# A hybrid encoder layer on one core: GpSimd's half of a sum put behind VectorE's, a small sum moved to GpSimd, one reciprocal a turn later

## The chip, the cores and the metric

The kernel runs on one core of a Trainium2 chip. The metric is the device time in microseconds (us) of one execution. Inside the core, TensorE (PE, with its weight loads as PEld), VectorE (DVE), ScalarE (ACT) and GpSimd (POOL) work in parallel, each through its own queue in order; SyncE (SP) issues all the DMAs here, in order too. An instruction that waits for another engine holds up everything behind it in its own queue.

## What is computed

One encoder layer is applied to two sequences with shared weights: a short one of 1024 tokens ("prompt") and a long one of 2048 ("sample"). The projected features go through three groups, each multiplied with its own SiLU gate, and their concatenation goes through an output projection, an RMS norm and a residual sum. Cut to what matters here:

```python
h = rms_norm(x, norm_pre)
z = h @ w_in                       # u_pool, g_pool, q, k, v, g_attn, q_x, g_x
pool_out = multiscale_pool(u_pool) * silu(g_pool)
# 8 query heads on 2 key/value heads, over all tokens
p = softmax(q @ k.T * 64 ** -0.5)
attn_out = (p @ v) * silu(g_attn)
# 4 heads over 256 memory tokens
x_out = memory_attention(q_x, k_m, v_m) * silu(g_x)
mix = concatenate([pool_out, attn_out, x_out])
y = mix @ w_out
out = x + rms_norm(y, norm_post)
```

All of it is float32; matrix products that need more than one pass' precision are split into a high and a low part (hi, lo), so that one product is three matmuls.

## The kernel before

The first part of the span, up to some 700 us, computes the projections of both sequences and stores queries, keys, values and gates to DRAM. The second part, which the change touches, is attention, output projection and the closing norm.

The second part goes through **pairs** of row blocks (256 tokens), eight of the sample and then four of the prompt. Each pair has three **groups**: kind 0 and kind 1 are self-attention on one key/value head each, kind 2 is the memory attention. After the first pair the order is 0, 2, 1. A group goes through its keys in **chunks** of 128 (16 in the sample, 8 in the prompt, 2 for the memory). Two chunks make a **turn**, and one loop over all turns of all groups writes out the order of every engine by hand (a manual schedule). Work that isn't tied to the loop is put into a table of due turns with `at(turn, f, ...)`, and `due(turn)` in the loop takes from it what is due; a fraction of a turn tells where inside the turn that is. In one turn the loop does:

- `look` (twice): TensorE computes a tile N of scores for a group to come (L186, L178 for the memory), and VectorE takes its negated row maxima (L191). The tile N has one buffer, so that the next N waits for this maximum. When all of a group are there, `shift` turns them into rows.
- `weights` (for two chunks): TensorE accumulates the scores S (L213, L221), and ScalarE takes the exponential into a tile P (L223). P has five buffers.
- `sums`: adds the chunk's P onto the group's z, column by column (L235 on GpSimd for the first 512 of 1024 columns, L236 on VectorE for the rest; `CUT = (0, 512)` says that in the prompt VectorE adds all of it). The first chunk of the turn is added in this turn, the second one in the next, between its two looks.
- `project`: one to four steps of the output projection of an earlier pair (`Output.piece`, L380 to L382, which read the tile mix).
- `values`: P times the values into acc (L248), every second turn for four chunks.
- `totals`: a turn after a group's last chunk, TensorE adds up z over the partitions (L257). It needs both halves of the last sum.

A group then goes on by due turns: `take` multiplies acc with the gate (L263, VectorE); `turned` and `inverse` transpose the totals, take the reciprocal (L272) and transpose back into a tile gz of one buffer (L267, L275, all VectorE), and store it to DRAM (L277); `spread` loads it back, broadcast over partitions (L282); `mix_out` multiplies the gated values with it (L292, GpSimd), and later ScalarE and GpSimd split the product into hi and lo (L295, L299) as the tile mix. The pooling branch of the pair goes through the same two lines as "pu". For the projected rows, `square` takes the sum of squares on ScalarE (L386), `scale` multiplies with the gain on VectorE (L398), `norm` makes the inverse root (L402 a sum of two numbers and epsilon on VectorE, L405 a power on GpSimd), and `out` scales and adds the residual (L414 on ScalarE and L415 on GpSimd; L411 on VectorE for the very last pair).

Of the kernel before, what the change touches and what calls it, by code (L numbers as in the profile page):

```python
# [10 lines left out]
ALU = mybir.AluOpType  # L11
# [6 lines left out]
EPS = 1e-6  # L18
# [5 lines left out]
def encoder(ctx, tc, I, O):  # L24


    nc = tc.nc
# [26 lines left out]
    make_identity(nc, ident)  # L54
    mhalf = const.tile([128, 8], F32, name="mhalf")
    nc.vector.memset(mhalf, -0.5)

    def rsqrt(pool, ss, n, count, tag):

        r = pool.tile([128, n], F32, name="rs", tag=tag)  # L60
        nc.vector.tensor_scalar(out=r, in0=ss, scalar1=1.0 / count, scalar2=EPS,  # L61
                                op0=ALU.mult, op1=ALU.add)
        nc.gpsimd.tensor_tensor(out=r, in0=r, in1=mhalf[:, 0:n], op=ALU.pow)  # L63
        return r
# [66 lines left out]
    class Group:  # L131
# [93 lines left out]
        def sums(self, k):  # L225
            if k == 0:
                return
            if k == 1:
                self.z = dbl.tile([128, 2, 512], F32, name="z", tag="z")
            flat = "p j q -> p (j q)"  # L230
            z, P = self.z.rearrange(flat), self.P[k].rearrange(flat)
            a = self.P[0].rearrange(flat) if k == 1 else z
            cut = CUT[self.s]
            if cut:
                nc.gpsimd.tensor_tensor(out=z[:, :cut], in0=a[:, :cut], in1=P[:, :cut], op=ALU.add)  # L235
            nc.vector.tensor_tensor(out=z[:, cut:], in0=a[:, cut:], in1=P[:, cut:], op=ALU.add)  # L236

        def values(self, ks):

# [107 lines left out]
    class Output:  # L347
# [51 lines left out]

        def norm(self):  # L400
            s1 = dbl.tile([128, 1], F32, name="s1", tag="s1")
            nc.vector.scalar_tensor_tensor(out=s1, in0=self.ss[:, 0:1], scalar=EPS, in1=self.ss[:, 1:2],  # L402
                                           op0=ALU.add, op1=ALU.add)
            self.r = dbl.tile([128, 1], F32, name="rs", tag="rsy")
            nc.gpsimd.tensor_tensor(out=self.r, in0=s1, in1=mhalf[:, 0:1], op=ALU.pow)  # L405

# [36 lines left out]
    later = {}  # L443

    def at(turn, f, *args):

        later.setdefault(round(turn, 2), []).append((f, args))
# [5 lines left out]
    first = {}  # L453
# [7 lines left out]
    for pair in pairs:  # L461
        ends = [first[g] + g.chunks // 2 - 1 for g in pair.groups]
        begin = first[pair.groups[0]]
        at(begin + 5.2, pair.load_pool)
        pair.free = begin + (6 if pair.last else HOLD[pair.s])
        at(begin + 7, pair.pool, begin + 7)
        for g in pair.groups:
            wait = first[g] + g.chunks // 2 + (2 if pair.last else 3)
            if pair is pairs[0] and g.kind != 1:
                wait += 3  # L470
            at(wait + 0.6, g.mix_out, wait + 1, pair)
        at(max(ends) + (3 if pair.last else 7), open_fill, pair)
    value_runs, sums_at = {}, {}
    for g in groups:
        n, c = first[g], g.chunks // 2
        g.early = g in pairs[0].groups
        at(n + (1.2 if g.kind == 1 and g.s == 0 else 0.2), g.load_late)
        k = 0
        while k < c:
            run = 1 if 2 < n + k < first[pairs[1].groups[0]] + 6 else 2  # L480
            value_runs[n + k + run - 1] = g, list(range(2 * k, min(2 * k + 2 * run, 2 * c)))
            k += run
        at(n + max(c, run) + 0.1, g.take)
        sums_at[n + c] = g
        at(n + c + 1.1, g.turned)
        if g in pairs[-1].groups:
            at(n + c + (1.4 if g.kind < 2 else 2.1), g.inverse)
            at(n + c + (1.4 if g.kind < 2 else 2.1), g.spread)
        else:
            at(n + c + (1.4 if g.kind < 2 else 2.6), g.inverse)  # L490
            at(n + c + (2.1 if g.kind < 2 else 3.1), g.spread)
    for c in range(NC):
        at(int(2.5 * c + 1), load_w_out, c)
        for h in range(2):
# [15 lines left out]
    looks, n = {}, len(turns)  # L510
# [31 lines left out]
    with ExitStack() as p1:  # L542
        one = p1.enter_context(tc.tile_pool(name="p1one", bufs=1))
# [437 lines left out]
    with tc.manual_schedule(engines=order):  # L981
        turn = 0
        while turn < len(turns) or later or fill:
            g, k = turns[turn] if turn < len(turns) else (None, 0)
# [66 lines left out]
```

## Time and profile before

| | before |
|---|---|
| median of 3 runs | 1746.3 us (1745.69 to 1746.43) |
| the profiled execution | 1745.43 us, span 1743.6 us |
| PE busy | 1697.3 us (97%) |
| DVE busy | 1116.8 us (64%) |
| POOL busy | 844.3 us (48%) |
| ACT busy | 656.7 us (38%) |
| granted TensorE clock, mean | 0.996 |

Read the rows of the profile like this. A row of a group has the line in the code, the engine, the operation, the tiles that it writes and reads with their shapes, the count, then the busy time in us and the mean in ns of one, and behind the second bar the engine's idle time just before them and what ended it. A row of the timeline begins with its start and its length in us; where rows in a row are equal they are merged ("x2"), and in square brackets stands the idle time of the engine before it and what ended that. A row of the waits names who waited for whom, then us in total, times, and the longest. A row of the windows has the stretch in us, its length, then the busy us of each engine with the count of instructions (PE, PEld, DVE, ACT, POOL), the granted TensorE clock, the share of the DMA engines and GB/s.

### The profile page before, as it was taken

What the parts mean: (1) busy time and instruction counts of PE and PEld (TensorE: products, weight loads), DVE (VectorE), ACT (ScalarE), POOL (GpSimd) and SP (SyncE); (2) the same over time, 40 slices, a digit from 0 to 9 for tenths busy, and PEclk for the clock granted to TensorE, in tenths of its full rate; (3) what the DMA queues carried; (4) which work ended last, traced back from release to release, by engine and by line L of the source; (5) the groups of instructions that cost most, each with busy time, mean ns of one, the idle gap of its engine ahead of it and who ended that gap; (6) DMA issues with size and microseconds to landing.
All of it is one profiled execution on the core that took longest, in us unless ns stands there. A gap on an engine that the chain in (4) does not pass through costs nothing. (4 is left out here: it accounts for less than half of the span.)

```text
span 1743.6 us, 25303 instructions
## 1 busy us (share of the span) xinstructions
PE 1697.3 (97%) x9400; PEld 1168.0 (67%) x9400; DVE 1116.8 (64%) x1434; ACT 656.7 (38%) x978; POOL 844.3 (48%) x778
## 2 busy tenths in 40 slices
PE   7899999999999999999999999999999999999998
PEld 6889889798898986544555555555555555566566
DVE  6754316552164424799878787877777757876862
ACT  5533225332252211445444344444343433443441
POOL 4555205570054610499666575767666663331331
PEclk9999999999999999999999999999999999999999
DMA  7643634436443393612121212112111143323222
GB/s 256 177 132 87 186 94 135 128 89 172 113 124 91 110 217 85 181 62 86 49 73 61 68 53 76 56 49 77 48 58 55 61 127 110 103 80 109 68 91 91
DMA packets 151851, 178.27 MB, mean 102 GB/s; under 512 B 20896, under 2 KB 120368, under 8 KB 151728
## 3 DMA queue, kind: packets, MB, share of 16 engines
q1 hardware_dynamic: 151728, 176.65, 34.0%
q8 instruction: 74, 1.21, 0.3%
q14 instruction: 49, 0.40, 0.1%
HBM read 121.26 MB, written 55.20 MB: 101 GB/s over the span
## 5 line engine op out<-in xcount | busy, mean ns | idle before, releaser
L191 DVE TENSOR_REDUCE nb<-N 128x2 f32<-128x1024 f32 x320 | 390.3, 1220 | 215.7 <-PE N L186 215.0
L223 ACT ACTIVATE P<-S 128x1024 f32<-128x1024 f32 x344 | 334.6, 1023 | 436.5 <-PE S L221 174.0
L235 POOL TENSOR_TENSOR z<-z,P 128x512 f32<-128x512 f32 x224 | 324.2, 1447 | 160.2 <-ACT P L223 140.4
L248 PE MATMUL acc<-P,V 128*64 128x512 f32 (+1 forms) x1472 | 320.3, 575 | 1.5
L236 DVE TENSOR_TENSOR z<-z,P 128x512 f32<-128x512 f32 (+1 forms) x272 | 269.3, 990 | 4.5 <-ACT P L223 4.3
L614 PE MATMUL pz<-hT_hi,w_hi 128*128 128x512 f32 x592 | 235.2, 397 | 1.7 <-ACT vmst L884 0.8
L615 PE MATMUL pz<-hT_lo,w_hi 128*128 128x512 f32 x592 | 232.8, 393 | 0.0
L616 PE MATMUL pz<-hT_hi,w_lo 128*128 128x512 f32 x592 | 231.5, 391 | 0.1
L248 PEld LDWEIGHTS acc<-P,V 128*64 128x64 f32 x1472 | 95.3, 137 | 170.7 <-issue 130.7
L221 PE MATMUL S<-q,DH 64*128 64x512 f32 x1280 | 201.6, 392 | 0.0
L63 POOL TENSOR_TENSOR rs<-rs,mhalf 128x4 f32<-128x4 f32 (+2 forms) x76 | 83.6, 1103 | 210.4 <-DVE rs L61 207.3
L186 PE MATMUL N<-KH,q 64*128 64x512 f32 x640 | 157.0, 487 | 12.4 <-DVE nb L191 11.0
L186 PEld LDWEIGHTS N<-KH,q 64*128 64x128 f32 x640 | 59.8, 183 | 153.2 <-DVE nb L191 86.4
L614 PE MATMUL pz<-w_hi,hT_hi 128*128 128x384 f32 (+1 forms) x416 | 141.6, 341 | 3.8 <-ACT hT_hi L68 3.8
L615 PE MATMUL pz<-w_lo,hT_hi 128*128 128x384 f32 (+1 forms) x416 | 140.7, 338 | 0.9 <-DVE w_lo L69 0.8
L616 PE MATMUL pz<-w_hi,hT_lo 128*128 128x384 f32 (+1 forms) x416 | 140.6, 339 | 0.0
L380 PE MATMUL py<-wo_hi,mix 128*128 128x512 f32 x336 | 139.0, 414 | 0.0
L69 DVE TENSOR_TENSOR w_lo<-wraw,w_hi 128x3072 fp32r<-128x3072 f32 (+2 forms) x21 | 67.8, 3227 | 107.3 <-ACT w_hi L68 106.9
L221 PEld LDWEIGHTS S<-q,DH 64*128 64x128 f32 x1280 | 120.1, 185 | 23.6 <-issue 2.4
L382 PE MATMUL py<-wo_hi,mix 128*128 128x512 f32 x336 | 131.6, 392 | 0.1
L381 PE MATMUL py<-wo_lo,mix 128*128 128x512 f32 x336 | 131.5, 391 | 0.0
L614 PEld LDWEIGHTS pz<-hT_hi,w_hi 128*128 128x128 f32 x592 | 111.1, 188 | 29.1 <-issue 4.5
(152 smaller groups left out, 2436.3 us busy)
## 6 DMA issues: line engine op xcount, KB each, us to landing
wraw<-w_in SPq DMA_DIRECT2D x15, 1536.0 KB
dg<-gst SPq DMA_DIRECT2D x48, 256.0 KB
q<-dq SPq DMA_DIRECT2D x24, 512.0 KB
gz<-rows SPq DMA_DIRECT2D x72, 128.0 KB
x<-x_sample SPq DMA_DIRECT2D x16, 512.0 KB
xr<-x_sample SPq DMA_DIRECT2D x16, 512.0 KB
y_sample<-xr SPq DMA_DIRECT2D x32, 256.0 KB
dq<-qst SPq DMA_DIRECT2D x96, 64.0 KB
```

The costliest lines, as they stand in the source:

```text
L186: nc.tensor.matmul(S[:, 512 * j:512 * j + 512], lhsT=self.q[h, 0, 128 * lane:128 * lane + 128], rhs=KH[self.kind][h, 512 * a:512 * a + 512 ...
L191: nc.vector.tensor_reduce(out=out, in_=S, axis=AX.X, op=ALU.max, negate=True)
L221: nc.tensor.matmul(S[:, at + x:at + x + w], lhsT=K, rhs=self.q[h, qx, x:x + w], start=False, stop=n == 2, skip_group_check=True)
L223: nc.scalar.activation(out=self.P[k].rearrange("p j q -> p (j q)"), in_=S, func=AF.Exp)
L235: nc.gpsimd.tensor_tensor(out=z[:, :cut], in0=a[:, :cut], in1=P[:, :cut], op=ALU.add)
L236: nc.vector.tensor_tensor(out=z[:, cut:], in0=a[:, cut:], in1=P[:, cut:], op=ALU.add)
L248: nc.tensor.matmul(self.acc[64 * j:64 * j + 64, x], lhsT=v, rhs=P[:, j, x], start=(k, i) == (0, 0), stop=k == self.chunks - 1, skip_group_ ...
L380: nc.tensor.matmul(ps, lhsT=mh, rhs=wo_hi[:, c, cols], start=first, stop=False)
L382: nc.tensor.matmul(ps, lhsT=ml, rhs=wo_hi[:, c, cols], start=False, stop=final)
L614: nc.tensor.matmul(ps, lhsT=sh, rhs=mh, start=c == 0, stop=False)
L615: nc.tensor.matmul(ps, lhsT=sh, rhs=ml, start=False, stop=False)
L616: nc.tensor.matmul(ps, lhsT=sl, rhs=mh, start=False, stop=c == n - 1)
```

## The change

It has three parts. In `sums`, VectorE's half is now issued first, and GpSimd's half is given a dependency on it, except for a group's last chunk. In `norm`, the sum of two numbers and epsilon is done by GpSimd's tensor_scalar, ahead of the power there. For the memory group of every pair, `inverse` comes 0.8 turns later and `spread` one turn later (not in the last pair), and `mix_out` one turn later (not in the first pair and not in the last).

```diff
+    def behind(later, first):
+        tc.add_manual_dep(later.ins, first.ins.name,
+                          mybir.DependencyInfo(mybir.DependencyClass.Sync, mybir.DependencyReason.DATA),
+                          reason="one after the other")
...
             cut = CUT[self.s]
+            v = nc.vector.tensor_tensor(out=z[:, cut:], in0=a[:, cut:], in1=P[:, cut:], op=ALU.add)
             if cut:
-                nc.gpsimd.tensor_tensor(out=z[:, :cut], in0=a[:, :cut], in1=P[:, :cut], op=ALU.add)
-            nc.vector.tensor_tensor(out=z[:, cut:], in0=a[:, cut:], in1=P[:, cut:], op=ALU.add)
+                e = nc.gpsimd.tensor_tensor(out=z[:, :cut], in0=a[:, :cut], in1=P[:, :cut], op=ALU.add)
+                if k < self.chunks - 1:
+                    behind(e, v)
...
             s1 = dbl.tile([128, 1], F32, name="s1", tag="s1")
-            nc.vector.scalar_tensor_tensor(out=s1, in0=self.ss[:, 0:1], scalar=EPS, in1=self.ss[:, 1:2],
-                                           op0=ALU.add, op1=ALU.add)
+            nc.gpsimd.tensor_scalar(out=s1, in0=self.ss[:, 0:1], scalar1=EPS, scalar2=self.ss[:, 1:2],
+                                    op0=ALU.add, op1=ALU.add)
...
             if pair is pairs[0] and g.kind != 1:
                 wait += 3
+            elif g.kind == 2 and not pair.last:
+                wait += 1
             at(wait + 0.6, g.mix_out, wait + 1, pair)
...
         else:
-            at(n + c + (1.4 if g.kind < 2 else 2.6), g.inverse)
-            at(n + c + (2.1 if g.kind < 2 else 3.1), g.spread)
+            at(n + c + (1.4 if g.kind < 2 else 3.4), g.inverse)
+            at(n + c + (2.1 if g.kind < 2 else 4.1), g.spread)
```

The lines of the changed kernel are some 5 to 7 higher than before's from `sums` on. In the rows below, a bracket names the engines or DMA queues whose semaphores the instruction waits for.

The first place is GpSimd's queue at the end of a kind 0 group of the sample, from the mix of the pair before to the group's last two chunks. Before:

```order
L299 TENSOR_TENSOR mix<-gate,mix 128x512 [waits Activation_49]
L405 TENSOR_TENSOR rs<-s_8859,mhalf 128x1 [waits DVE_49]
L235 TENSOR_TENSOR z<-z,P 128x512 [waits Pool_49]
L235 TENSOR_TENSOR z<-z,P 128x512 [waits Activation_49,Pool_49]
L415 TENSOR_TENSOR xr<-xr,y 128x512 [waits DMAHW1_49,DMAHW6_49,DMAHW0_49,Activation_49]
L299 TENSOR_TENSOR mix<-gate,mix 128x512 x2
L292 TENSOR_TENSOR pu<-pu,pg 128x512 [waits DMAHW7_49,DMAHW1_49,DMAHW0_49]
L235 TENSOR_TENSOR z<-z,P 128x512 [waits Pool_49]
L235 TENSOR_TENSOR z<-z,P 128x512 [waits Activation_49,Pool_49]
L415 TENSOR_TENSOR xr<-xr,y 128x512 [waits Activation_49]
L235 TENSOR_TENSOR z<-z,P 128x512 [waits Pool_49]
```

And of the change:

```order
L306 TENSOR_TENSOR mix<-gate,mix 128x512 [waits Activation_49]
L409 TENSOR_SCALAR s_8859<-ssy 128x1
L412 TENSOR_TENSOR rs<-s_8859,mhalf 128x1 [waits Pool_49]
L241 TENSOR_TENSOR z<-z,P 128x512 [waits DVE_49]
L241 TENSOR_TENSOR z<-z,P 128x512 [waits DVE_49,Pool_49]
L422 TENSOR_TENSOR xr<-xr,y 128x512 [waits DMAHW1_49,DMAHW6_49,DMAHW0_49,Activation_49]
L306 TENSOR_TENSOR mix<-gate,mix 128x512 x2
L299 TENSOR_TENSOR pu<-pu,pg 128x512 [waits DMAHW7_49,DMAHW1_49,DMAHW0_49]
L241 TENSOR_TENSOR z<-z,P 128x512 [waits DVE_49,Pool_49] x2
L422 TENSOR_TENSOR xr<-xr,y 128x512 [waits Activation_49]
L241 TENSOR_TENSOR z<-z,P 128x512 [waits Pool_49]
```

The instructions keep their order; the small sum stands ahead of the power, and every sum but the last of the group waits for VectorE instead of ScalarE.

The second place is VectorE's queue behind the first chunks of the kind 1 group of the sample's last pair, where the memory group's reciprocal (RECIPROCAL, STREAM_TRANSPOSE gz) stands. Before:

```order
L236 TENSOR_TENSOR z<-P 128x512
L236 TENSOR_TENSOR z<-z,P 128x512 x3
L272 RECIPROCAL rz<-rz 128x8
L275 STREAM_TRANSPOSE gz<-rz 128x256
L191 TENSOR_REDUCE nb<-N 128x2
L236 TENSOR_TENSOR z<-z,P 128x512
L191 TENSOR_REDUCE nb<-N 128x2
L236 TENSOR_TENSOR z<-z,P 128x512
L191 TENSOR_REDUCE nb<-N 128x2
```

And of the change:

```order
L239 TENSOR_TENSOR z<-P 128x512
L239 TENSOR_TENSOR z<-z,P 128x512 x3
L196 TENSOR_REDUCE nb<-N 128x2
L239 TENSOR_TENSOR z<-z,P 128x512
L196 TENSOR_REDUCE nb<-N 128x2
L239 TENSOR_TENSOR z<-z,P 128x512
L279 RECIPROCAL rz<-rz 128x8
L282 STREAM_TRANSPOSE gz<-rz 128x256
L196 TENSOR_REDUCE nb<-N 128x2
```

Two row maxima and two sums now stand ahead of the reciprocal. In SyncE's queue the load of gz (two DMAs) goes behind the load of a following group's queries, here also behind two loads of keys.

The third place is VectorE's queue in the prompt's second pair, where the norm's small sum (s) stood ahead of a row maximum. Before:

```order
L236 TENSOR_TENSOR z<-P 128x1024
L191 TENSOR_REDUCE nb<-N 128x2
L272 RECIPROCAL rz<-rz 128x8
L275 STREAM_TRANSPOSE gz<-rz 128x256
L402 SCALAR_TENSOR_TENSOR s_13557<-ssy 128x1
L191 TENSOR_REDUCE nb<-N 128x2
```

And of the change:

```order
L239 TENSOR_TENSOR z<-P 128x1024
L196 TENSOR_REDUCE nb<-N 128x2
L279 RECIPROCAL rz<-rz 128x8
L282 STREAM_TRANSPOSE gz<-rz 128x256
L196 TENSOR_REDUCE nb<-N 128x2
```

The sum is gone from VectorE, and nothing else moved there.

## The prediction

> **What bounds the kernel now.** I read the page's busy shares first, then its groups.
>
> ```profile
> span 1743.6 us, 25303 instructions
> PE 1697.3 (97%) x9400; PEld 1168.0 (67%) x9400; DVE 1116.8 (64%) x1434; ACT 656.7 (38%) x978; POOL 844.3 (48%) x778
> L235 POOL TENSOR_TENSOR z<-z,P 128x512 f32<-128x512 f32 x224 | 324.2, 1447 | 160.2 <-ACT P L223 140.4
> ```
>
> TensorE is busy 97% of the span, so only what TensorE waits for can move the time. GpSimd's halves of the sums of weights (L235; VectorE's are L236) cost 324 us on an engine that is not the bound. The next view is TensorE's own waits, stage by stage: first between 830 and 1420 us, the long sequence's attention from the second pair of row blocks on, then between 715 and 830 us.
>
> ```profile
> engine line waited for: us in total, times, longest us
> PE acc L257 <- POOL z L235: 1.1, 4, 0.6
> ```
> ```profile
> PE N L186 <- DVE nb L191: 3.8, 7, 1.2
> ```
>
> In 590 us of steady state TensorE waits 1.1 us in all, and the one thing that it waits for is GpSimd's half of a sum (L257 adds up the finished sums). For VectorE it isn't shown waiting once. A faster VectorE therefore has nothing to win in these 590 us, and a later GpSimd has something to lose. Only in the first two groups of heads does TensorE wait for VectorE's row maxima, 3.8 us together.
>
> **Part 1: GpSimd's half behind VectorE's half.** The claim behind such an order would be that the halves disturb each other. They do:
>
> ```profile
> 1004.30 0.68 DVE L236 TENSOR_TENSOR z<-z,P 128x512 f32<-128x512 f32 x1
> ...
> 1009.53 0.68 DVE L236 TENSOR_TENSOR z<-z,P 128x512 f32<-128x512 f32 x1
> ...
> 1011.61 1.69 DVE L236 TENSOR_TENSOR z<-z,P 128x512 f32<-128x512 f32 x1
> ```
>
> VectorE's add takes 0.68 us when it comes first, and 1.69 us at 1011.61, where a GpSimd add is already running. GpSimd's queue in the same stretch, the end of one group (chunks 8 to 15 of its sum), is this:
>
> ```profile
> 999.26 2.99 POOL L235 TENSOR_TENSOR z<-z,P 128x512 f32<-128x512 f32 x2 [1.64 <-ACT P L223]
> 1004.47 1.64 POOL L235 TENSOR_TENSOR z<-z,P 128x512 f32<-128x512 f32 x1 [2.21 <-PE N L186]
> 1006.07 1.77 POOL L299 TENSOR_TENSOR mix<-pu,mix 128x512 fp32r<-128x512 f32 x1
> 1007.80 1.29 POOL L299 TENSOR_TENSOR mix<-gate,mix 128x512 fp32r<-128x512 f32 x1
> 1009.05 0.55 POOL L405 TENSOR_TENSOR rs<-s,mhalf 128x1 f32<-128x1 f32 x1
> 1009.55 3.19 POOL L235 TENSOR_TENSOR z<-z,P 128x512 f32<-128x512 f32 x2
> 1012.80 1.65 POOL L415 TENSOR_TENSOR xr<-xr,y 128x512 f32<-128x512 f32 x1
> 1014.41 2.97 POOL L299 TENSOR_TENSOR mix<-gate,mix 128x512 fp32r<-128x512 f32 x2
> 1017.33 1.27 POOL L292 TENSOR_TENSOR pu<-pu,pg 128x512 f32<-128x512 f32 x1
> 1018.56 3.12 POOL L235 TENSOR_TENSOR z<-z,P 128x512 f32<-128x512 f32 x2
> 1021.63 1.75 POOL L415 TENSOR_TENSOR xr<-xr,y 128x512 f32<-128x512 f32 x1
> 1023.35 1.28 POOL L235 TENSOR_TENSOR z<-z,P 128x512 f32<-128x512 f32 x1
> ```
> ```profile
> 927.69 1.28 POOL L235 TENSOR_TENSOR z<-z,P 128x512 f32<-128x512 f32 x1
> ```
> ```profile
> 929.03 0.64 PE L257 MATMUL acc<-z,ones 128*32 128x256 f32 x8
> ```
> ```profile
> 1024.68 0.64 PE L257 MATMUL acc<-z,ones 128*32 128x256 f32 x8 [0.19 <-POOL z L235]
> ```
> ```profile
> 1407.30 0.64 PE L257 MATMUL acc<-z,ones 128*32 128x256 f32 x8 [0.56 <-POOL z L235]
> ```
>
> From 1004.47 to the last add's end at 1024.63 GpSimd doesn't stop, and 0.05 us later TensorE starts L257, after an idle 0.19 us. This is the place without slack. It lies at the end of the first group of a pair and comes back every 96 us: the first and the last of six such starts, at 929 us (0.06 us behind GpSimd's add, too short a wait to be listed) and at 1407 us, are shown beside the one at 1024.
>
> Now the change. Chunk 9's GpSimd add is the second of the two from 999.26; it is finished by 1002.25, in time that GpSimd otherwise idles (the 2.21 us ahead of 1004.47). Behind VectorE's half, which ends at 1004.98, it starts at about 1005.1. So the busy stretch starts 0.6 us later (1005.1 against 1004.47) and has 1.25 us more in it (one add, 1.28 us, less its overlap with the next). Part 2 puts a small sum ahead of rs, some 0.35 us. That adds 2.2 us. Taken off: thirteen big instructions at 1.28 us and rs at 0.55 us would be 17.2 us, and the rows from 1004.47 sum to 20.5 us, so some 3.3 us of them is waiting for VectorE. Most of it stays, since VectorE's six adds still have to get in between. Laid out one by one, with 1.28 us for each GpSimd instruction and 0.55 us more where a VectorE add gets in first, the last add ends near 1026.1, so 1.5 us later than now. I take **+1.5 us** for each of six ends, **+9.0 us**; the bounds are 0 (all the added time given back by fewer collisions) and 2.2 us (none), 0 to 13.2 us. The last chunk is left free by the change, but it stands behind the others in GpSimd's queue, so that doesn't help.
>
> What else stands behind the delayed adds: mix (L299) and xr (L415). TensorE's projection reads the first two mix rows, the second of them two of its steps of three matmuls in:
>
> ```profile
> 1010.10 0.50 PE L380 MATMUL py<-wo_hi,mix 128*128 128x512 f32 x1
> ```
>
> They end at 1007.84 and 1009.09 and by the same lay-out come up to 1.6 us and 2.2 us later, 1009.4 and 1011.3. That is about in time, and I cost it at nothing; were the second needed at 1010.10 itself, it would be 1.2 us per pair. Buffers of weights come free later too:
>
> ```profile
> ACT P L223 <- POOL z L235: 102.8, 35, 3.9
> ```
>
> ScalarE's exponentials are named as waiting 102.8 us for GpSimd's adds. As TensorE isn't shown waiting for ScalarE once between 830 and 1420 us, that cover holds for another us or two; cost nothing.
>
> The gain of part 1 is in the first two groups: at most the 4.1 us there (3.8 us above and one more wait of 0.3 us of the same sort). In them L257 again needs GpSimd's last add, and GpSimd's queue is full, so most of an earlier VectorE is given back there; I take **-0.8 us**, bounds 0 and -4.1.
>
> The Trainium skill ("SBUF — State Buffer", section "Who interferes with whom") says that VectorE and GpSimd hold a shared port in turn for a whole instruction, and that the issue order decides who blocks. The rows agree (0.68 against 1.69 us). By that rule the order moves the waiting from one engine to the other and frees no port time, and here the engine without slack is the one that is now put second; the sum would be nearer the 13.2 us than 9.0.
>
> **Part 2: the norm's small sum on GpSimd.** It removes 24 instructions from VectorE and adds 24 to GpSimd. GpSimd has no such instruction now; the nearest rows are the power on the same 128x1 shape and a 128x8 product:
>
> ```profile
> L405 POOL TENSOR_TENSOR rs<-s,mhalf x24: 541/548/1540, 866.1 to 1738.5; 128x1 f32<-128x1 f32 x24
> ```
> ```profile
> L811 POOL TENSOR_TENSOR sm<-sm,edge 128x8 f32<-128x8 f32 x4 | 0.8, 202 | 0.2
> ```
>
> So between 0.20 and 0.55 us; I take 0.35, which is already in the stretch above. On VectorE it matters in two places, in the short sequence:
>
> ```profile
> 1553.25 1.08 DVE L402 SCALAR_TENSOR_TENSOR s<-ssy 128x1 f32<-128x1 f32 x1
> ```
> ```profile
> 1555.52 0.50 PE L186 MATMUL N<-KH,q 64*128 64x512 f32 x2 [0.89 <-DVE nb L191]
> ```
> ```profile
> 1619.73 0.50 PE L186 MATMUL N<-KH,q 64*128 64x512 f32 x2 [0.84 <-DVE nb L191]
> ```
>
> The sum, held up by GpSimd, delays the maximum behind it by 1.0 us, and TensorE idles 0.89 us; the same 64 us later, 0.84 us. Without it: **-1.7 us**.
>
> At the very end the sum stands behind two products on VectorE:
>
> ```profile
> 1736.79 0.19 ACT L386 ACTIVATION_READ_ACCUMULATOR junk<-py 128x1 f32 x1
> ```
> ```profile
> 1737.63 0.68 DVE L398 TENSOR_TENSOR y<-py,npost 128x512 f32<-128x512 f32 x1
> ...
> 1739.10 1.41 DVE L411 SCALAR_TENSOR_TENSOR xr<-y,rs,xr 128x512 f32<-128x512 f32 x2 [0.73 <-POOL rs L405]
> ```
>
> Its input is there at 1736.98. GpSimd, idle, could add (0.35) and take the power (0.55) by about 1738.0, so L411 starts near 1738.1 instead of 1739.10: **-1.0 us** (0.8 to 1.1 with the sum's bounds).
>
> **Part 3: the memory group's reciprocal a turn later.** Its instructions (reciprocal, transpose, one store, two loads, the product on GpSimd) keep their number and their spacing. What goes is a wait of VectorE for GpSimd's product of the group before:
>
> ```profile
> DVE gz L275 <- POOL gate L292: 4.1, 1, 4.1
> ```
> ```profile
> 1426.22 0.66 PE L186 MATMUL N<-KH,q 64*128 64x512 f32 x2 [2.24 <-DVE nb L191]
> ```
> ```profile
> 1426.40:1429.80 3.40, 3.40 (x10) 1.01 (x11) 3.02 (x3) 0.00 (x0) 0.74 (x1) 0.50 0.36 92
> ```
>
> The transpose L275 waits 4.1 us, the row maxima behind it are late, TensorE idles 2.24 us, and for the next 3.4 us its granted clock is 0.50, which loses half of 3.4 us. In the new order two maxima and two adds stand ahead of the reciprocal, so this stall goes whole: 2.2 + 1.7 = **-3.9 us**. In SyncE's queue the reload of gz now stands behind loads of keys and queries; the product that waits for it has nothing on TensorE behind it, so I cost it at nothing.
>
> The Trainium skill ("TensorE: Matmul & The Clock Gate", section "What's actually happening") lets the clock fall after at least one idle window of about 3.4 us. By it 2.24 us would not do, and the 1.7 us would not be gained; here the row with 0.50 decides. Another stall shows how near the edge this is:
>
> ```profile
> 328.52 0.66 PE L820 MATMUL pm<-sm,poolw 128*128 128x504 f32 x1 [2.19 <-DVE u L781]
> ```
> ```profile
> 328.50:331.90 3.40, 3.38 (x13) 2.52 (x14) 1.51 (x4) 1.06 (x3) 0.00 (x0) 1.00 0.29 60
> ```
>
> After 2.19 us idle the clock stayed at 1.00.
>
> **The sum.** +9.0 - 0.8 - 1.7 - 1.0 - 3.9 = **+1.6 us**. The profiled execution took 1745.43 us (1.8 us beside its span), 0.9 us under the median of 1746.3; on the median that is **1747.9 us**.
>
> **The rivals.** A measurement of this kernel can tell about 0.2%, 3.5 us, from no change.
> - *GpSimd catches up* (faster). If fewer collisions give back all that is added to the 20 us stretch, or if VectorE nearly always starts first already, as at 1009.53 against 1009.55, the +9.0 falls away: 1746.3 - 7.4 = 1738.9 us. For it: GpSimd's adds average 1447 ns against 1.28 us undisturbed. Against it: VectorE's six adds must still fit into the stretch.
> - *GpSimd's last add becomes TensorE's wait* (slower). Each of six ends gives the full 2.2 us, and idle times of over 2 us at L257 halve the clock at two of them, 1.7 us each: 1746.3 + 13.2 + 3.4 - 7.4 = 1755.5 us. It decides against the change from 7.4 / 6 = 1.2 us per end on. For it: L257 has no slack now. Against it: the clock held at 2.19 us idle. By the clock rule of the Trainium skill above neither the halving here nor the 1.7 us of part 3 would be there, and this case would be 1753.8 us.
>
> **How the numbers follow.** The balance (1743 to 1750) gets 0.42, GpSimd catching up 0.25, the full delay 0.33. With one case to each band: faster 0.25, same 0.42, slower 0.33. The unknowns' ends are 1746.3 - 10.7 (nothing lost, all 4.1 us gained) = 1735.6 and 1746.3 + 13.2 + 3.4 - 4.7 (0.8 at the end, 1.7 in the short sequence and only the 2.2 us) = 1758.2; leaving a tenth out on each side, the range is 1738 to 1756.
>
> **What would show it.** Right: VectorE's L236 adds near 0.7 us, GpSimd's adds near 1.3 us; TensorE idle for 1.5 us or more ahead of L257 six times, 96 us apart; no stall near 1426, 1555 and 1620; the last L411 pair some 0.6 us behind the product. Wrong: L257's waits unchanged at 0.2 us (then I mis-sized GpSimd's stretch), or TensorE waiting at L299's mix or for ScalarE's weights (then the cover that I counted on was thin).

## The result and the profile after

| | before | after |
|---|---|---|
| median | 1745.99 us (1743.88 to 1746.43, 4 runs) | 1768.65 us (1768.06 to 1772.95, 4 runs) |
| the profiled execution | 1745.43 us, span 1743.6 us | 1768.06 us, span 1766.3 us |
| mean granted TensorE clock | 0.996 | 0.990 |

The ratio is 1.0137 [1.0118, 1.0156]: the change makes the kernel slower by 1.4%, 22.7 us. The page of the changed kernel, in the rows that answer to those of before (the lines are 3 to 9 higher now: L241 is GpSimd's half of a sum, L239 VectorE's, L264 the totals, L306 the mix):

```profile
PE 1707.1 (97%) x9400; PEld 1175.8 (67%) x9400; DVE 1091.6 (62%) x1410; ACT 657.3 (37%) x978; POOL 818.3 (46%) x802
L241 POOL TENSOR_TENSOR z<-z,P 128x512 f32<-128x512 f32 x224 | 293.3, 1309 | 172.4 <-DVE z L239 159.2
```

This page alone looks like a success. GpSimd's adds fell from 1447 to 1309 ns, VectorE is busy for 25 us less, GpSimd for 26 us less. The gain of VectorE is not where the order was to bring it, though. Its adds by shape, before and after:

```profile
L236 DVE TENSOR_TENSOR z<-z,P 128x512 f32<-128x512 f32 x224 | 201.6, 900 | 4.0 <-ACT P L223 4.0
L236 DVE TENSOR_TENSOR z<-P 128x512 f32<-128x512 f32 x24 | 28.7, 1194 | 0.0
```
```profile
L239 DVE TENSOR_TENSOR z<-z,P 128x512 f32<-128x512 f32 x224 | 200.1, 893 | 4.5 <-ACT P L228 4.4
L239 DVE TENSOR_TENSOR z<-P 128x512 f32<-128x512 f32 x24 | 15.9, 661 | 0.0
```

Only the first add of each group became short (1194 to 661 ns, 12.8 us together). The other 224 take 893 ns instead of 900, and most of what is left of the 25 us are the small sums, which have gone to GpSimd. So what the order shortened are GpSimd's adds, and of VectorE's only the first of each group. The first two experiments below agree: in these two rows VectorE has 892 and 663 ns with the order alone, 859 and 1196 ns without it.

TensorE's waits over the whole span (who waited for whom; us in total, times, longest) show where the span went:

```profile
PE acc L264 <- POOL z L241: 13.3, 6, 2.7
PE N L191 <- DVE nb L196: 7.0, 13, 1.3
PE py L264 <- POOL z L241: 3.8, 2, 2.2
...
PE py L389 <- POOL mix L306: 2.9, 1, 2.9
```

The wait for GpSimd's last add of a group, 1.1 us in four waits before, is now 13.3 us in six; two more such waits (in the first pair, where the totals go into the tile py) and one for mix are new. GpSimd's queue at the same place as in the prediction, chunks 9 to 15 of a kind 0 group's sum, now reads:

```profile
1017.73 1.28 POOL L241 TENSOR_TENSOR z<-z,P 128x512 f32<-128x512 f32 x1 [2.56 <-DVE z L239]
1019.71 1.28 POOL L241 TENSOR_TENSOR z<-z,P 128x512 f32<-128x512 f32 x1 [0.69 <-DVE z L239]
...
1024.05 0.30 POOL L409 TENSOR_SCALAR s<-ssy 128x1 f32<-128x1 f32 x1
1024.44 0.84 POOL L412 TENSOR_TENSOR rs<-s,mhalf 128x1 f32<-128x1 f32 x1
1025.25 2.65 POOL L241 TENSOR_TENSOR z<-z,P 128x512 f32<-128x512 f32 x2
...
1033.71 2.98 POOL L241 TENSOR_TENSOR z<-z,P 128x512 f32<-128x512 f32 x2
1036.66 1.26 POOL L422 TENSOR_TENSOR xr<-xr,y 128x512 f32<-128x512 f32 x1
1037.89 1.25 POOL L241 TENSOR_TENSOR z<-z,P 128x512 f32<-128x512 f32 x1
```
```profile
1039.20 0.64 PE L264 MATMUL acc<-z,ones 128*32 128x256 f32 x8 [2.12 <-POOL z L241]
```

Chunk 9's add (1017.73) now waits for VectorE and opens the busy stretch. Chunk 10's add waits for VectorE once more, 0.69 us, and from 1019.71 to 1039.14 GpSimd hardly stops. TensorE starts the totals 0.06 us later, after 2.12 us idle, where it was 0.19 us. Of VectorE's adds in that stretch some are still held up, as the slowest and the one right before the stretch show:

```profile
1016.88 0.68 DVE L239 TENSOR_TENSOR z<-z,P 128x512 f32<-128x512 f32 x1
...
1033.75 1.80 DVE L239 TENSOR_TENSOR z<-z,P 128x512 f32<-128x512 f32 x1
```

The order binds the two halves of one chunk, not VectorE's add of one chunk against GpSimd's instructions of another. The add at 1033.75 is that of chunk 15 and still meets GpSimd's of chunk 13, which began at 1033.71.

The stall has an echo. The stretches right after it (length; busy us and count of PE, PEld, DVE, ACT, POOL; granted clock; DMA share; GB/s) at this end and at the next:

```profile
1040.20:1043.60 3.40, 3.40 (x20) 2.42 (x16) 2.75 (x4) 1.02 (x1) 0.18 (x1) 0.51 0.72 218
1139.20:1142.60 3.40, 3.40 (x20) 2.40 (x16) 2.75 (x4) 1.02 (x1) 0.16 (x1) 0.50 0.70 224
```

For 3.4 us the clock is half. The starts of the same instructions in both traces give the price: from the totals at 1024.68 (now 1039.20, +14.52) to those five microseconds later (1029.65, now 1045.71, +16.06) another 1.54 us go. This came at five of the six ends.

With such differences of starts the whole span can be put together:

| stretch | us | |
|---|---|---|
| first part, to 717 us | +2.1 | not the change's, see below |
| first pair and start of the second, to 833 us | +8.9 | totals late by 1.64 and 2.17 us, mix by 2.88 us, two half clocks |
| six ends of kind 0 groups | +11.1 | 1.77 to 2.06 each, from 40 us ahead of the totals to their start |
| half clocks behind five of them | +7.7 | 1.53 to 1.55 each |
| stall at 1426 us | -3.9 | gone |
| short sequence, two stalls | -1.8 | gone (0.95 and 0.88) |
| the very end | -1.0 | |
| small steps elsewhere | -0.4 | |
| sum | +22.6 | span 1743.63 to 1766.26 (the rounded rows give 22.7) |

The loss of the second pair has a place of its own. GpSimd before the mix, in the changed kernel:

```profile
808.42 1.28 POOL L241 TENSOR_TENSOR z<-z,P 128x512 f32<-128x512 f32 x1 [0.69 <-DVE z L239]
810.38 1.29 POOL L241 TENSOR_TENSOR z<-z,P 128x512 f32<-128x512 f32 x1 [0.69 <-DVE z L239]
...
813.61 1.26 POOL L241 TENSOR_TENSOR z<-z,P 128x512 f32<-128x512 f32 x1 [0.69 <-DVE z L239]
815.56 1.28 POOL L241 TENSOR_TENSOR z<-z,P 128x512 f32<-128x512 f32 x1 [0.69 <-DVE z L239]
...
827.82 1.26 POOL L306 TENSOR_TENSOR mix<-pu,mix 128x512 fp32r<-128x512 f32 x1
```
```profile
829.13 0.80 PE L389 MATMUL py<-wo_hi,mix 128*128 128x512 f32 x1 [2.88 <-POOL mix L306]
```

Four times GpSimd stands idle for 0.69 us, the length of VectorE's half, with a full queue behind it: 2.8 us. TensorE, which needs the mix at the queue's end, waits 2.88 us. In the kernel before, GpSimd's rows of this stretch show no idle time:

```profile
809.72 3.48 POOL L235 TENSOR_TENSOR z<-z,P 128x512 f32<-128x512 f32 x2
...
817.83 1.29 POOL L299 TENSOR_TENSOR mix<-pu,mix 128x512 fp32r<-128x512 f32 x1
```

### The profile page after: what moved, and what is told of

It reads as the page before. It is cut to its first block, busy times and chain, and to the rows that moved or that the text cites. A ratio compares the mean times of both kernels' runs of the same rounds, so it can differ in the third digit from the quotient of the medians.

```text
span 1766.3 us, 25311 instructions
## 1 busy us (share of the span) xinstructions
PE 1707.1 (97%) x9400; PEld 1175.8 (67%) x9400; DVE 1091.6 (62%) x1410; ACT 657.3 (37%) x978; POOL 818.3 (46%) x802
## 5 line engine op out<-in xcount | busy, mean ns | idle before, releaser
L241 POOL TENSOR_TENSOR z<-z,P 128x512 f32<-128x512 f32 x224 | 293.3, 1309 | 172.4 <-DVE z L239 159.2
L239 DVE TENSOR_TENSOR z<-z,P 128x512 f32<-128x512 f32 (+1 forms) x272 | 265.5, 976 | 5.1 <-ACT P L228 4.7
L226 PE MATMUL S<-q,DH 64*128 64x512 f32 x1280 | 206.3, 400 | 0.0
```

The costliest lines, as they stand in the source:

```text
L226: nc.tensor.matmul(S[:, at + x:at + x + w], lhsT=K, rhs=self.q[h, qx, x:x + w], start=False, stop=n == 2, skip_group_check=True)
L239: v = nc.vector.tensor_tensor(out=z[:, cut:], in0=a[:, cut:], in1=P[:, cut:], op=ALU.add)
L241: e = nc.gpsimd.tensor_tensor(out=z[:, :cut], in0=a[:, :cut], in1=P[:, :cut], op=ALU.add)
```

## The experiments

The theory at this point: part 1, the order, makes GpSimd's last adds late and brings all of the loss; parts 2 and 3 gain, except that the small sum lengthens GpSimd's queue a little. The rivals: part 2's small sum (on the full GpSimd) carries the loss; or part 3 has moved work into these places; or the loss is in the last chunks' order alone.

### Parts 2 and 3 without the order

Diff against the kernel before (with part 3 as in the change):

```diff
-            nc.vector.scalar_tensor_tensor(out=s1, in0=self.ss[:, 0:1], scalar=EPS, in1=self.ss[:, 1:2],
-                                           op0=ALU.add, op1=ALU.add)
+            nc.gpsimd.tensor_scalar(out=s1, in0=self.ss[:, 0:1], scalar1=EPS, scalar2=self.ss[:, 1:2],
+                                    op0=ALU.add, op1=ALU.add)
...
+            elif g.kind == 2 and not pair.last:
+                wait += 1
```

> Parts 2 and 3 alone: the sums of weights as before, no order between the halves. Theory (the order makes GpSimd's last add of a group late, TensorE waits for it at the totals, and some of these waits halve its clock): the waits at the six ends go back to 0.2 to 0.6 us, with 0.3 us each for the small sum on GpSimd, no half clock between 830 and 1420 us; the gains of the two parts (3.9, 1.8 and 1.0 us) stay: about 1741 us (1738 to 1744), faster than before by 0.2 to 0.4%. Rival (the small sum and the later product fill GpSimd's queue and have their share of the loss): 1752 us or more, with waits of over 1 us at the totals.

Measured: 1741.74 us (1740.53 to 1743.25, 10 runs), ratio 0.9984 [0.9975, 0.9993]. The stall at 1426 us is gone (3.87 us), no half clock stands behind a totals, and the totals wait for GpSimd:

```profile
PE acc L262 <- POOL z L240: 3.9, 6, 1.0
```

3.9 us in six against 1.1 in four. That is the small sum: 0.38 to 0.44 us at each end (the run below that takes it out of these places bears this out). So it is neither part 2 nor part 3 that makes the kernel slow, but part 2 gives back a good part of what it gains.

### The order alone

Diff against the kernel before: the new `sums` and `behind` of the change, nothing else.

> Part 1 alone: VectorE's half first and GpSimd's half behind it except for a group's last chunk; norm and reciprocals as before. Theory: the whole loss is here, and the gains of the other parts are missing: 1768.65 + 6.7 less some 2 us for the small sum that is not on GpSimd, about 1773 us (1769 to 1777), waits of 1.7 us or more at the totals, and the stall of the memory group's reciprocal near 1440 us is back. Rival (the parts need each other): 1758 us or less.

Measured: 1775.96 us (1773.37 to 1776.59, 4 runs), ratio 1.0175 [1.0159, 1.019]. Part 1 carries the loss, and alone it is worse than all three parts together. In the steady stretch (840 to 1445 us) TensorE's waits are:

```profile
PE acc L264 <- POOL z L241: 10.2, 6, 2.3
PE N L191 <- DVE nb L196: 9.4, 6, 1.6
```

The totals wait 1.57 to 1.60 us (the last 2.28), not 2.1, since the small sum isn't in GpSimd's queue. That is a little under the 1.7 us expected, and there is no half clock behind any of the six. But a second stall has come, once in every pair:

```profile
1060.41 0.45 DVE L282 STREAM_TRANSPOSE gz<-rz 128x256 f32<-128x256 f32 x1 [2.60 <-POOL gate L299]
```

It is the stall that the kernel before had only at 1426 us: VectorE's transpose waits for GpSimd's product of the group before, the row maxima behind it are late, and TensorE waits 1.57 us for them. The order delays that product in every pair. So part 3, which moves the transpose back by a turn, is what makes part 1 bearable; in the full change this stall is nowhere (part 2 is missing here too, but neither the transpose nor that product is part of it). At the place of the old stall TensorE now idles 3.07 us, with 6.83 us of half clock behind it. The time lies in the expected range partly by luck: the 7.7 us of half clock behind the totals are gone, and the 9.4 us of the second stall, which nothing had foretold, stand in their place. VectorE's half issued first, but without the dependency, was not run; the rows name the dependency, since it is VectorE's half that ends 159.2 of the 172.4 us of idle time before GpSimd's adds in the full change.

### The order in the first half of each sum

```diff
-                if k < self.chunks - 1:
+                if k < self.chunks // 2:
```

> The change, but with the order only for the first half of a group's chunks (1 to 7 of 16; none in the memory group). Theory (what counts is that GpSimd's adds of the last chunks can't be done ahead of its busy stretch): the last chunks are free, the waits at the six steady ends fall from 2.1 to 2.7 us to 0.6 us or less, no half clock there, and at least half of the 8.9 us of the first two pairs goes: 1741 to 1750 us. Rival (each ordered add costs its share through the waits on VectorE): half of the loss stays, about 1757 us.

Measured: 1748.5 us (1744.76 to 1750.45, 10 runs), ratio 1.002 [1.001, 1.003]. The steady ends are where the kernel of parts 2 and 3 has them (0.57 to 0.58 us, the last 0.97, no half clock), so the steady loss comes from the order on the last chunks. One part of the expectation was a miss: at least half of the early 8.9 us should have gone, and most of it stayed (1.76, 1.92 and 3.98 us, 7.7 together). From 715 to 1445 us:

```profile
PE acc L264 <- POOL z L241: 3.9, 6, 1.0
PE py L264 <- POOL z L241: 3.3, 2, 1.6
PE py L389 <- POOL mix L306: 2.9, 1, 2.9
```

From the first pair to the start of the second GpSimd also splits the output weights (wo_lo), and in the kernel of parts 2 and 3 it shows no idle time between 802 and 828 us in which a delay of early chunks could be made up. That this keeps the early loss is argued from those rows, not tested apart.

### The order in the first pair only

```diff
-                if k < self.chunks - 1:
+                if self.early and k < self.chunks - 1:
```

> The change, but with the order only in the first pair's three groups, where TensorE does wait for VectorE. Theory: the six steady ends are free again; in the first pair the waits at the totals (1.6 and 2.2 us in the change) stay, and with them a half clock: 1741 + 4 to 7 us, 1745 to 1749 us. Rival (the first pair's stalls in the change come from elsewhere, as the chain of projections, and the order helps VectorE there): 1741 us or less, with no wait at the first pair's totals.

Measured: 1746.51 us (1743.45 to 1750.35, 10 runs), ratio 1.0008 [0.9998, 1.0017], 4.8 us above the kernel of parts 2 and 3 on the same chip. The first pair's two late totals stay (1.64 and 2.16 us, the second with a half clock behind it), the mix is on time and the steady ends are at 0.56 to 0.61 us (the last 0.97). So the order costs in the first pair too, at the very place where VectorE's relief was to help. And the 2.88 us at the mix come from the order on the second pair's chunks, which this run leaves free.

### The change with 384 of 1024 columns on GpSimd

```diff
-    CUT = (0, 512)
+    CUT = (0, 384)
```

> The change as it is, but GpSimd adds 384 of 1024 columns instead of 512, VectorE 640. Theory (the length of GpSimd's queue from VectorE's half to a group's last add sets the wait at the totals): seven adds of some 1.28 us in the stretch become some 0.3 us shorter, 2.1 us, which is what TensorE waits there; the six steady waits fall below 0.7 us, their half clocks go, the first two pairs keep some of their loss: 1768.65 less some 18, about 1750 us (1745 to 1754). Rival (the semaphore hop and VectorE's being late set it, whatever the size): 1765 us or more with waits near 2 us.

Measured: 1753.45 us (1747.6 to 1753.98, 5 runs), ratio 1.0036 [1.0023, 1.005]. Shorter adds on GpSimd take the loss down to a third (7.6 of 22.7 us), as they should if the length of its queue is the cause. The size was a miss: the steady waits are 1.26 to 1.28 us (the last 1.88), not under 0.7. Only the last one has a half clock behind it.

### The order left out, the small sum on GpSimd only in the short sequence

Against the kernel of parts 2 and 3:

```diff
-            nc.gpsimd.tensor_scalar(out=s1, in0=self.ss[:, 0:1], scalar1=EPS, scalar2=self.ss[:, 1:2],
-                                    op0=ALU.add, op1=ALU.add)
+            if self.s == 0:
+                nc.gpsimd.tensor_scalar(out=s1, in0=self.ss[:, 0:1], scalar1=EPS, scalar2=self.ss[:, 1:2],
+                                        op0=ALU.add, op1=ALU.add)
+            else:
+                nc.vector.scalar_tensor_tensor(out=s1, in0=self.ss[:, 0:1], scalar=EPS, in1=self.ss[:, 1:2],
+                                               op0=ALU.add, op1=ALU.add)
```

> No order; the reciprocal later; the norm's small sum on GpSimd only in the short sequence, on VectorE in the long one (part 3, and part 2 where the profile showed a gain). Theory: in the run with parts 2 and 3 alone the six waits at the totals grew from some 0.2 to 0.58 us because of the small sum in GpSimd's queue, 0.4 us each; they go back to 0.2 us: 1741.7 - 2.4, about 1739.4 us (1738 to 1741). Rival (the later product does it): no change against that run.

Measured: 1739.96 us (1738.91 to 1741.39, 6 runs), ratio 0.997 [0.9958, 0.9982]: faster than both kernels. The steady waits for GpSimd are the old ones again:

```profile
PE acc L262 <- POOL z L240: 1.3, 5, 0.6
```

The gains are 3.9 us at 1426, 0.9 us at one of the two stalls of the short sequence and 1.02 us at the end. The other stall (0.89 us) stays: the norm there still belongs to rows of the long sequence, so that its small sum is on VectorE. Against the kernel of parts 2 and 3, run on another chip, the intervals overlap; which of the two is faster stays open, though the waits say this one.

### The same with 384 columns on GpSimd from the second pair on

```diff
-            cut = CUT[self.s]
+            cut = CUT[self.s] if self.early else min(CUT[self.s], 384)
```

> As the run before in this list, but with 384 columns on GpSimd from the second pair on. Theory: the waits at the six totals go to nothing, 0.2 us each and 0.6 us at the last, and VectorE's longer halves stay hidden: 1738 us (1737 to 1740). Rival (VectorE, 0.13 us longer for each add, becomes what TensorE waits for): 1742 us or more, with TensorE waiting for the row maxima L191's successors in the steady state.

Measured: 1741.54 us (1739.19 to 1743.85, 8 runs), ratio 0.9974 [0.9963, 0.9984]: nothing further, against an expectation of 1738 (1737 to 1740). The rival's mechanism is there, at a time just below its 1742 us. TensorE waits for GpSimd no more in the steady stretch, but now waits for VectorE, which has the other columns:

```profile
PE N L183 <- DVE top L196: 3.0, 6, 0.5
```

1.3 us of waits for one engine became 3.0 us for the other. Of the two sizes tried, 512 of 1024 columns is no worse; sizes between them were not run.

## Why the prediction was wrong

The forecast was a balance, 1747.9 us in 1738 to 1756, and the time came out at 1768.65. By its own terms:

- **The six ends** (+9.0): the mechanism was right, the size a little low. Each end lost 1.8 us, not 1.5, 11.1 in all; the bound of 13.2 held. By the two first experiments the order makes some 1.4 us of an end and the small sum 0.4. What the lay-out lacked is the idle 0.69 us ahead of 1019.71: it took the stretch as unbroken from chunk 9's add on, but chunk 10's add waits for VectorE too. The Trainium skill ("SBUF — State Buffer", section "Who interferes with whom") says that the issue order decides who blocks; the prediction took from it that the order frees no time, and put the sum by that at nearer 13.2. The measured 11.1 lies half way between 9.0 and 13.2. That collisions remain is shown by VectorE's add of 1.80 us at 1033.75 and by the mean of 893 ns, where the prediction's sign of being right was "near 0.7 us".
- **The half clock behind them** (0 in the forecast, two of six in the slower rival): five of six, 7.7 us. One step that failed is "the clock held at 2.19 us idle", one case taken for an edge. Five of the stalls here were shorter than that one (2.07 to 2.14 us; the last was 2.72), and four of the five still halved the clock.
- **The first two groups** (-0.8, bounds 0 and -4.1): +8.9 us up to the second pair, the largest miss and the other step that failed. The prediction wrote that L257 needs GpSimd's last add there too and that GpSimd's queue is full, and then used it only to shrink the gain. The same two facts made a late add a wait of TensorE, as at the steady ends. The gain didn't come either: TensorE's waits for row maxima from 717 to 860 us are as before (3.8 us in seven):

```profile
PE N L191 <- DVE nb L196: 3.7, 7, 1.0
```

- **Mix** (about in time, costed at nothing, else 1.2 us per pair): right from the third pair on, wrong in the second, where TensorE waited 2.88 us and a half clock followed; both are within the +8.9 us above.
- **Weights' buffers** (nothing): right. TensorE isn't shown waiting for a tile P anywhere.
- **Part 2**: the small sum takes 0.30 us at best and 0.38 in the mean (0.35 taken); the short sequence gained 1.83 us (1.7 taken), the end 1.03 (1.0). The last rows show it: sum, power, and the scaling 0.04 us behind it.

```profile
1760.75 0.30 POOL L409 TENSOR_SCALAR s<-ssy 128x1 f32<-128x1 f32 x1 [1.80 <-ACT junk L393]
1761.13 0.56 POOL L412 TENSOR_TENSOR rs<-s,mhalf 128x1 f32<-128x1 f32 x1
```
```profile
1761.73 1.42 DVE L418 SCALAR_TENSOR_TENSOR xr<-y,rs,xr 128x512 f32<-128x512 f32 x2
```

- **Part 3** (-3.9): 3.9 us went, stall and half clock both.
- **The first part** wasn't in the sum, and the change doesn't touch it: 2.1 us, of which 1.6 is a half clock at 330 us. It comes behind the same 2.19 us stall that the kernel before has at 328 us, and five of the nine traces have it; the section on the hardware says why. Against the kernel before, the first part lies between -0.6 and +2.9 us in the traces of the experiments.

The differences to the terms are 9.7 (first pairs), 7.7 (clock), 2.1 (size of the ends) and 2.1 us (first part); with -0.1 in the short sequence and -0.4 of small steps that is the 21 us between the forecast's +1.6 and +22.6. The slower rival had the right mechanism at the six ends and in the clock. Its price had 2.1 us too much at the ends, and it was short by the same 9.7 us at the first pairs and by 4.3 of the clock's 7.7; the range was short for the same two reasons.

## What to carry to other kernels

Before putting one engine behind another, look at which of the two the bound engine waits for, and whether its queue has idle time there: TensorE's only steady wait was for GpSimd, and the order spent GpSimd's slack to keep the halves of a chunk apart. That made GpSimd's instructions shorter and its last one later. Busy time and mean durations can all get better while the time gets worse, so read the waits of the bound engine, stage by stage, first. And count a stall of TensorE of 1.8 us and more as one that may cost some 1.5 us more in clock.

## What the runs showed of the hardware

The half clock comes in spells of one step of 3.41 us, now and then of two, that all begin on one grid of 3.413 us, fixed through an execution. In the changed kernel the starts at 1040.2 and 1139.2 us are 29 steps apart. By these traces what counts is the idle time inside one step of this grid, not the length of a stall. Each pair below is such a step and the one behind it in the changed kernel: the end at 941.77 (idle 2.14 us), the end at 1039.20 (2.12 us), and the stall of the first part (2.19 us):

```profile
937.80:941.21 3.41, 1.83 (x8) 1.14 (x7) 1.46 (x2) 0.69 (x2) 3.41 (x3) 1.00 0.00 0
941.21:944.62 3.41, 2.85 (x28) 1.96 (x28) 1.73 (x3) 0.74 (x1) 1.75 (x2) 1.00 0.49 156
1036.79:1040.20 3.41, 1.28 (x14) 0.55 (x14) 0.00 (x0) 0.69 (x2) 3.41 (x3) 1.00 0.20 77
1040.20:1043.61 3.41, 3.41 (x20) 2.42 (x16) 2.75 (x4) 1.02 (x1) 0.18 (x1) 0.51 0.72 217
326.86:330.27 3.41, 1.29 (x4) 0.80 (x5) 2.94 (x7) 0.83 (x3) 1.44 (x2) 1.00 0.18 42
330.27:333.68 3.41, 3.41 (x10) 2.63 (x9) 0.58 (x1) 0.60 (x1) 0.00 (x0) 0.50 0.38 82
```

The stall at 941.77 is cut by the grid: 1.58 us of idle in the first step, 0.56 in the second, and no half clock follows. The 2.12 and 2.12 us that the other two steps hold are each followed by one. In the kernel before the same stall of the first part was cut, too:

```profile
323.94:327.35 3.41, 2.39 (x11) 1.63 (x9) 2.81 (x3) 0.37 (x1) 3.17 (x4) 1.00 0.91 294
327.35:330.77 3.42, 2.25 (x8) 1.59 (x9) 2.67 (x6) 0.90 (x3) 0.48 (x1) 1.00 0.18 39
330.77:334.18 3.41, 3.41 (x16) 2.83 (x16) 0.00 (x0) 0.16 (x1) 0.00 (x0) 1.00 0.31 66
```

So "the clock held at 2.19 us" was a matter of where the grid fell, and some 1.6 us of what one execution differs from another could come from it. Worked out so over the nine traces after 100 us, for steps that ran at the full clock, those with 1.78 us of idle or more were followed by a half clock, those with up to 1.63 us never; the edge is about half a step. One such step speaks against it, with 1.9 us of idle and the full clock behind it, in the kernel with the order alone:

```profile
755.50:758.90 3.40, 1.53 (x8) 0.20 (x4) 1.05 (x1) 0.90 (x2) 3.32 (x3) 1.00 0.00 0
758.90:762.30 3.40, 1.91 (x20) 1.27 (x22) 0.79 (x1) 0.03 (x1) 2.67 (x3) 1.00 0.00 0
```

What sets that one apart stays open; no run varied the idle time of a step by itself. Nor does the edge hold everywhere: ahead of 100 us a step with 1.49 us of idle was followed by a half clock (the change with 384 columns), and in the kernel with the order alone a step already at half clock, with 0.66 us of idle from 1455.31 on, was followed by a second one. The Trainium skill ("TensorE: Matmul & The Clock Gate", "What's actually happening") asks for a whole window of about 3.4 us idle; the window's length agrees with the 3.41 us here, the whole of it does not, since some 1.8 us within one were enough.
